# The adaLN gate's multiply-accumulates spread over twelve of sixteen column tiles, with fewer buffers

## The chip, the cores and the metric

One NeuronCore of a Trainium2 chip runs the whole program. The time is that of one execution on the device in microseconds (us), the median of several runs. Engines in the text: TensorE (PE in the rows, PEld its weight loads), VectorE (DVE), ScalarE (ACT), GpSimd (POOL), and SyncE (SP), which issues the DMAs one after the other.

## The reference

One layer of a hybrid sequence model runs on 640 tokens (512 latent, 128 context), 2048 channels wide. The part around the change:

```python
mod = jax.nn.silu(cond) @ p['ada_w'] + p['ada_b']
shift, scale, gate = jnp.split(mod, 3, axis=-1)
xm = rms_norm(x, p['norm_g']) * (1 + scale[:, None]) + shift[:, None]
# mixer: z = xm @ w_in, two scans, then
y_a = (y_rwkv * silu(g_a)) @ p['w_out_a']
y_b = ((h_f + h_bk) * silu(g_b)) @ p['w_out_b']
merged = jax.nn.sigmoid(m_a) * y_a + jax.nn.sigmoid(m_b) * y_b
out = merged @ p['w_out']
x = x + gate[:, None] * out
```

The condition `cond` is one vector for the latent tokens and one for the context tokens, so `gate` is a product of a 2048 x 2048 matrix with two vectors. It is needed only after the last product.

## The kernel before

Everything lies with channels on the 128 partitions and the 640 tokens along the row. All products run in a split form: weights and data are each parted into a high and a low half, and three matmuls (high x high, high x low, low x high) make one product. A weight block `wr` of 128 x 512 comes in by DMA (`fetch`, L297); ScalarE copies each half-tile of 256 columns to `wh` (L309), GpSimd subtracts to get `wl` (L310). `split` keeps five such half-tiles ahead of TensorE, and there are three `wr` buffers. `piece` (L327 in it) issues the matmuls of one block of 128 rows of the weight and then calls `tick`, which advances the generators in the list `side` by one step each. A product of eight blocks so gives eight ticks. The schedule is written out by hand: each engine executes its instructions in the order in which this code emits them.

The stage of the change is that of the sixteen merged column tiles, n = 0 to 15. For each n two old tiles `thx` of 128 x 640 (the stored tanh of the merge gates) are loaded (L1347, L1348), then come the product b(n) of eight blocks with `w_b`, its eviction L1350 on VectorE, the product a(n) with `w_a`, its eviction L1352, the sum L1353, the copy to the high half `xh` on ScalarE (L1355) and the subtraction to the low half `xl` on VectorE (L1356). Two PSUM buffers `pj` hold the products. The two tiles `xh`, `xl` of each n are the data of the last product with `w_o`, which follows the stage.

Ahead of the stage two merge-gate products run; the second half of the last one is evicted by ScalarE into `g` (L1234) six ticks later, inside b(0).

The generator `gates` runs at the side of this stage. It works out the adaLN gate as 64 pairs of multiply-accumulates on VectorE: four quarters h of the 2048 inputs, sixteen tiles n of 128 outputs. For a pair a tile `gws` of 128 x 512 of the transposed weight (256 KB, `ada_g`) is loaded into a ring (L1300), and VectorE multiplies it with the Silu of the condition `cb` (128 copies of 512 inputs for each of two conditions, L1304 loads it, L1309 applies Silu on ScalarE) and sums along the row: L1314 for the first condition, L1316 for the second. Each profile row of them is followed by a short read of the accumulator. A pair takes two ticks, so a tile of the stage has eight pairs, and the gate runs over eight tiles. Its buffers lie in the pool `gp`, on the bytes that the second half of the `xh`, `xl` tiles takes up later. At n = 8 what is left of the generator is emitted at once and the pool is closed.

Of the kernel before, what the change touches and what calls it, by code (L numbers as in the profile page):

```python
# [9 lines left out]
F32 = mybir.dt.float32  # L10
F32R = mybir.dt.float32r
AF = mybir.ActivationFunctionType
ALU = mybir.AluOpType
# [3 lines left out]
P = 128  # L17
D = 2048
KT = D // P
# [16 lines left out]
GK = D // 4  # L36
# [14 lines left out]
X3 = (3, 2, 2, 2, 3, 1, 2, 1)  # L51
NI = (1, 2, 1, 1)

BI, BP, EP = 7, 0.8, 0.5
RMS_EPS = 1e-6
GN_EPS = 64e-5
DECAY = math.exp(-0.5)
# [77 lines left out]
def step_kernel(ctx: ExitStack, tc: tile.TileContext, xt, w_in, w_a, w_b, w_o, ws, lw2, ada_w, ada_g, ada_b, cond, condr, gains,  # L135
                par, gw, s0, cst, y_out, s_out, h_out):
    nc = tc.nc
    V, S, G, PE = nc.vector, nc.scalar, nc.gpsimd, nc.tensor
# [65 lines left out]
    side, back, front, waiting = [], [], [], []  # L204
# [12 lines left out]
    def step(queue):  # L217
        while queue:
            try:
                next(queue[0])  # L220
                return
            except StopIteration:
                queue.pop(0)
# [10 lines left out]
    def idle(n):  # L234
        for _ in range(n):
            yield
# [31 lines left out]
    for i in range(NT):  # L268
        n = NM[i] if i < NT - 1 else 2 * KT - nm - M_AFTER
# [61 lines left out]
    def product(key, xs, cuts=(0, HT, T), ps=None):  # L331
        js = jobs[key]
        if ps is None:
            ps = ps2()
            hs = [(ps[:, s], a, b) for s, (a, b) in enumerate(zip(cuts, cuts[1:]))]
        else:
            hs = [(p, a, b) for p, a, b in zip(ps, cuts, cuts[1:])]
        for n, j in enumerate(js):
            piece(j, xs, hs, 4 * n, 4 * len(js))
        return ps  # L340

    def halves(t):
        return t[:, :T].rearrange("p (a b) -> p a b", a=2)
# [16 lines left out]
    def operand(pool, k):  # L360
        xs.append((pool.tile([P, T], F32R, name=f"xh{k}"), pool.tile([P, T], F32R, name=f"xl{k}")))
# [36 lines left out]
    with tc.tile_pool(name="start", bufs=1) as st, tc.tile_pool(name="ps", bufs=2, space=PSUM) as sp:  # L398
# [34 lines left out]
        for s in range(2):  # L433
            h = slice(s * HT, (s + 1) * HT)
# [270 lines left out]
    with tc.tile_pool(name="rwkv", bufs=1) as rp:  # L705
# [523 lines left out]
        def merge_gate(j, pool=mpool, bufs=1):  # L1229
            ps = product(("m", j), xs)  # L1230

            def half(s):
                t = pool.tile([P, HT], F32, tag="g", name="g", bufs=bufs)
                S.activation(t, ps[:, s, :HT], AF.Tanh, scale=0.5)  # L1234
                later(1, lambda: nc.sync.dma_start(thm[j][:, s * HT:(s + 1) * HT], t))

            half(0)
            later(6, lambda: half(1))
# [22 lines left out]
    with tc.tile_pool(name="outp", bufs=1) as op:  # L1261
        ab_ = {}

        def branches():
            todo = [(n, src[i], i) for n, src in (("b", ybd), ("a", yad)) for i in range(NT)]
            held = []

            def load():
                if todo:
                    n, src, i = todo.pop(0)  # L1270
                    t = op.tile([P, T], F32, tag="yr", name="yr", bufs=6)
                    nc.sync.dma_start(t, src)
                    held.append((n, i, t))

            for _ in range(5):
                load()
            yield from idle(BI)
            while held:
                n, i, t = held.pop(0)
                h, lo = op.tile([P, T], F32R, name=f"y{n}h{i}"), op.tile([P, T], F32R, name=f"y{n}l{i}")  # L1280
                S.activation(h, t, AF.Copy)
                V.tensor_tensor(lo, t, h.bitcast(F32), ALU.subtract)
                ab_[n, i] = (h, lo)
                load()
                yield

        def gates():

            gs = op.tile([P, 4, KT, 2], F32, name="gs")
            cb = [gp.tile([P, 2, GK], F32, name=f"cb{h}") for h in range(4)]  # L1290
            ring = [gp.tile([P, GK], F32, name=f"gws{n}") for n in range(6)]
            junk = gp.tile([P, GK], F32, name="junk")
            todo = [(h, n) for h in range(4) for n in range(KT)]
            held = []

            def load():
                if todo:
                    h, n = todo.pop(0)
                    w = ring[(h * KT + n) % len(ring)]
                    nc.sync.dma_start(w, ada_g[h, n])  # L1300
                    held.append((h, n, w))

            for h in range(4):
                nc.sync.dma_start(cb[h], condr[h:h + 1].to_broadcast([P, 2, GK]))  # L1304
            for _ in range(len(ring) - 1):
                load()
            yield from idle(4)
            for h in range(4):
                S.activation(cb[h], cb[h], AF.Silu)  # L1309
                yield  # L1310
            while held:
                h, n, w = held.pop(0)
                load()
                V.scalar_tensor_tensor(junk, w, 1.0, cb[h][:, 0], ALU.mult, ALU.mult, accum_out=gs[:, h, n, 0:1])  # L1314
                yield
                V.scalar_tensor_tensor(w, w, 1.0, cb[h][:, 1], ALU.mult, ALU.mult, accum_out=gs[:, h, n, 1:2])  # L1316
                yield
            V.tensor_tensor(gs[:, 0:2], gs[:, 0:2], gs[:, 2:4], ALU.add)
            V.tensor_tensor(gs[:, 0], gs[:, 0], gs[:, 1], ALU.add)
            V.tensor_tensor(mod[:, 2], gs[:, 0], adb[:, 2].unsqueeze(2).to_broadcast([P, KT, 2]), ALU.add)  # L1320

        pace[:] = [0.0, BP]
        side.append(branches())
        for k in range(M_AFTER):
            merge_gate(2 * KT - M_AFTER + k, op, 4)
        while side:
            step(side)

        pace[:] = [0.0, 1.0]
        xstack.close()  # L1330
        del xs[:]
        first_half = ctx.enter_context(tc.tile_pool(name="merged0", bufs=1, side="right"))
        for k in range(KT // 2):
            operand(first_half, k)
        gstack = ExitStack()
        gp = gstack.enter_context(tc.tile_pool(name="gp", bufs=1, side="right"))
        side.append(gates())
        for n in range(KT):
            if n == KT // 2:
                while side:  # L1340
                    step(side)
                gstack.close()
                second_half = ctx.enter_context(tc.tile_pool(name="merged1", bufs=1, side="right"))
                for k in range(KT // 2, KT):
                    operand(second_half, k)
            ta, tb = (op.tile([P, T], F32, tag="yr", name="thx", bufs=6) for _ in range(2))
            nc.sync.dma_start(ta, thm[n])  # L1347
            nc.sync.dma_start(tb, thm[KT + n])  # L1348
            ps = product(("b", n), [ab_["b", i] for i in range(NT)])
            V.scalar_tensor_tensor(halves(tb), halves(tb), 1.0, ps[:, :, :HT], ALU.add, ALU.mult)  # L1350
            ps = product(("a", n), [ab_["a", i] for i in range(NT)])
            V.scalar_tensor_tensor(halves(ta), halves(ta), 1.0, ps[:, :, :HT], ALU.add, ALU.mult)  # L1352
            V.tensor_tensor(ta, ta, tb, ALU.add)  # L1353
            h, lo = xs[n]
            S.activation(h, ta, AF.Copy)  # L1355
            V.tensor_tensor(lo, ta, h.bitcast(F32), ALU.subtract)  # L1356
# [79 lines left out]
```

## Time and profile before

| | |
|---|---|
| median of 3 runs | 2256.55 us (2256.01 to 2258.0) |
| the profiled execution | 2254.77 us, its span 2253.0 us |
| TensorE busy | 2111.6 us, 94% of the span |
| VectorE busy | 1365.5 us, 61% |
| ScalarE busy | 976.4 us, 43% |
| GpSimd busy | 874.2 us, 39% |
| mean granted TensorE clock | 0.975 of full |
| moved by DMA | 281.64 MB |

The span runs from the first to the last instruction of the profiled execution; 1.77 us lie around it. Busy shares are means over the whole program, whose stages have different limits, so they do not tell what bounds one stage. TensorE's busy time holds pipelined matmuls with modelled ends.

### The profile page before, as it was taken

How to read it: one execution, taken by the hardware profiler on the slowest of the kernel's cores; microseconds unless marked ns; L12 is line 12 of the kernel's file. 1: busy time of each engine (PE TensorE's matmuls, PEld its weight loads, DVE VectorE, ACT ScalarE, POOL GpSimd, SP SyncE). 2: the span in 40 equal slices, each digit the busy share in tenths (PEclk: the TensorE clock that was granted, in tenths of full speed). 3: DMA queues.
4: the chain of work that ended last, by engine and by line, in shares of the span. 5: the costliest groups of instructions: out<-in, count | busy, mean ns of one | idle time of the engine just before them, and what ended most of it. 6: DMA issues, size and time to landing. Idle time of an engine off the chain costs nothing.

```text
span 2253.0 us, 47526 instructions
## 1 busy us (share of the span) xinstructions
PE 2111.6 (94%) x18236; PEld 1968.6 (87%) x18236; DVE 1365.5 (61%) x2665; ACT 976.4 (43%) x2264; POOL 874.2 (39%) x1164
## 2 busy tenths in 40 slices
PE   3999999999999998999989989989999888999997
PEld 2789999998888898888988988979888888999997
DVE  5555765687656676676466666764614798223364
ACT  4346776543444344334433444344335212234554
POOL 1244554553333433323333333334324445443343
PEclk8999999999999999999999999999999999999999
DMA  9953333323322223223222222232224765344474
GB/s 336 348 170 127 127 114 121 101 93 88 94 75 83 70 81 95 62 75 97 80 83 71 80 86 68 71 110 73 86 77 161 254 207 176 117 145 155 156 236 153
DMA packets 203507, 281.64 MB, mean 125 GB/s; under 512 B 69360, under 2 KB 91056, under 8 KB 202768
## 3 DMA queue, kind: packets, MB, share of 16 engines
q1 hardware_dynamic: 202832, 277.38, 38.5%
q8 instruction: 144, 2.36, 0.4%
q0 software_dynamic: 448, 1.23, 0.2%
q14 instruction: 83, 0.68, 0.1%
HBM read 237.70 MB, written 39.85 MB: 123 GB/s over the span
## 4 chain that ended last, share of the span: by engine, by line
PE 72%; DVE 19%; DMA 5%; issue 2%; ACT 1%; SPq 1%; POOL 0%; DVEq 0%; ACTq 0%; POOLq 0%
PE pj L327 53%; DVE tmp L1072 3%; DVE xi L1074 3%; DVE junk L1314 3%; PE rw L563 3%; DVE gws L1316 2%; PE rw L479 2%; PE rw L930 2%; DVE st L954 1%; PE pj L479 1%; PE ada L381 1%; PE rw L1153 1%; PE rw L1141 1%; PE rw L948 1%; PE rw L1166 1%
## 5 line engine op out<-in xcount | busy, mean ns | idle before, releaser
L310 POOL TENSOR_TENSOR wl<-wr,wh 128x256 fp32r<-128x256 f32 x922 | 789.6, 865 | 1289.0 <-ACT wh L309 1202.7
L327 PE MATMUL pj<-xh,wh 128*128 128x320 f32 (+2 forms) x2976 | 762.3, 323 | 2.6 <-ACT wh L309 2.5
L327 PE MATMUL pj<-xh,wl 128*128 128x320 f32 (+2 forms) x2976 | 726.2, 311 | 2.0 <-DVE wl L310 1.5
L327 PE MATMUL pj<-xl,wh 128*128 128x320 f32 (+2 forms) x2976 | 724.8, 311 | 0.0
L309 ACT ACTIVATE wh<-wr 128x256 fp32r<-128x256 f32 x1048 | 421.3, 413 | 521.5 <-PE pj L327 394.6
L327 PEld LDWEIGHTS pj<-xh,wh 128*128 128x128 f32 x2976 | 503.3, 190 | 34.5 <-issue 14.2
L327 PEld LDWEIGHTS pj<-xh,wl 128*128 128x128 f32 x2976 | 513.5, 190 | 4.0 <-DVE wl L310 2.5
L327 PEld LDWEIGHTS pj<-xl,wh 128*128 128x128 f32 x2976 | 513.8, 190 | 0.1
L1072 DVE TENSOR_TENSOR tmp<-xn,xi 104x30 f32<-104x30 f32 (+14 forms) x240 | 101.7, 424 | 82.3 <-ACT xn L1067 75.7
L1001 DVE COPY sv<-rw 64x128 f32<-64x128 f32 x80 | 23.6, 295 | 199.3 <-ACT sv L1000 198.1
L310 DVE TENSOR_TENSOR wl<-wr,wh 128x256 fp32r<-128x256 f32 x126 | 58.1, 462 | 126.1 <-ACT wh L309 126.0
L1074 DVE TENSOR_TENSOR xi<-xi,tmp 104x30 f32<-104x30 f32 (+14 forms) x240 | 99.9, 416 | 8.2
L327 PE MATMUL pj<-ybh,wh 128*128 128x320 f32 x256 | 62.5, 327 | 21.7 <-DVE thx L1350 21.7
L327 PEld LDWEIGHTS pj<-ybh,wh 128*128 128x128 f32 x256 | 45.9, 202 | 23.5 <-issue 23.5
L1314 DVE SCALAR_TENSOR_TENSOR junk<-gws,cb 128x512 f32<-128x512 f32 x64 | 61.5, 960 | 6.4 <-DMA gws<-ada_g 6.4
L954 DVE TENSOR_TENSOR st<-rw,c 64x512 f32<-64x512 f32 (+1 forms) x96 | 57.6, 600 | 12.4 <-PE rw L948 10.2
L327 PE MATMUL pj<-yah,wh 128*128 128x320 f32 x256 | 59.2, 313 | 6.1 <-DVE thx L1350 4.1
L327 PE MATMUL pj<-ybh,wl 128*128 128x320 f32 x256 | 61.8, 324 | 0.0
L327 PE MATMUL pj<-ybl,wh 128*128 128x320 f32 x256 | 61.8, 324 | 0.0
L327 PE MATMUL pj<-yah,wl 128*128 128x320 f32 x256 | 59.4, 313 | 0.9 <-POOL wl L310 0.9
L1316 DVE SCALAR_TENSOR_TENSOR gws<-gws,cb 128x512 f32<-128x512 f32 x64 | 58.4, 913 | 2.2
L1355 ACT ACTIVATE xh<-thx 128x640 fp32r<-128x640 f32 x16 | 11.8, 740 | 109.8 <-DVE thx L1353 103.4
(766 smaller groups left out, 3102.2 us busy)
## 6 DMA issues: line engine op xcount, KB each, us to landing
wr<-w_in SPq DMA_DIRECT2D x312, 256.0 KB
adaw<-ada_w SPq DMA_DIRECT2D x64, 512.0 KB
wr<-w_o SPq DMA_DIRECT2D x128, 256.0 KB
gws<-ada_g SPq DMA_DIRECT2D x64, 256.0 KB
thl<-th SPq DMA_DIRECT2D x32, 320.0 KB
th<-thl SPq DMA_DIRECT2D x32, 320.0 KB
thm<-g SPq DMA_DIRECT2D x64, 160.0 KB
thx<-thm SPq DMA_DIRECT2D x32, 320.0 KB
```

The costliest lines, as they stand in the source:

```text
L309: S.activation(h, r, AF.Copy)
L310: lows[pos[1] % len(lows)].tensor_tensor(lo, r, h.bitcast(F32), ALU.subtract)
L327: PE.matmul(p[:, :t1 - t0], w, x[:, t0:t1], start=(k == 0 and a == 0), stop=(k == nk - 1 and a == 2))
L479: PE.matmul(p[:, :HT], u[:, w], x[:, t], start=new, stop=end)
L563: PE.matmul(p, a, b, start=(n == 0), stop=(n == 2))
L930: PE.matmul(pa[hd(e), x:x + P], z.bk[d][hd(e), n, e], st4s[d][hd(e), n, e].rearrange("p a t -> p (a t)"), start=True, stop=True)
L954: V.tensor_tensor(st4s[d][so, n0:n0 + nn, e], pb[so, :m].rearrange("p (c a t) -> p c a t", a=2, t=CH), mb[so], ALU.mult)
L1001: V.tensor_copy(sv[hd(1), a, 1], src[hd(1), b])
L1072: V.tensor_tensor(t, xn[:NV, j, j + 1:].unsqueeze(2).to_broadcast([NV, m, j]), xi[:NV, j, :j].unsqueeze(1).to_broadcast([NV, m, j]), ALU.mult)
L1074: V.tensor_tensor(xi[:NV, j + 1:, :j], xi[:NV, j + 1:, :j], t, ALU.add)
L1314: V.scalar_tensor_tensor(junk, w, 1.0, cb[h][:, 0], ALU.mult, ALU.mult, accum_out=gs[:, h, n, 0:1])
L1316: V.scalar_tensor_tensor(w, w, 1.0, cb[h][:, 1], ALU.mult, ALU.mult, accum_out=gs[:, h, n, 1:2])
```

## The change

The generator takes three ticks for a pair instead of two (`GI = (2, 2)`: two steps after the second multiply-accumulate, for even and for odd n), and the stage gives it twelve tiles instead of eight. The `xh`, `xl` tiles are parted into twelve and four, and the gate's buffers lie on the bytes of the last four. They hold four `gws` instead of six and two `cb` instead of four: the first condition is loaded and put through Silu at the start, the next ones during the quarter before. The first multiply-accumulate follows the first Silu without a step between. Lines below the change have numbers higher by seven in the changed code (L1350 is L1357 there).

```diff
--- before.py
+++ after.py
@@ -51,7 +51,7 @@
 X3 = (3, 2, 2, 2, 3, 1, 2, 1)
 NI = (1, 2, 1, 1)
 
-BI, BP, EP = 7, 0.8, 0.5
+BI, BP, EP, GI = 7, 0.8, 0.5, (2, 2)
 RMS_EPS = 1e-6
 GN_EPS = 64e-5
 DECAY = math.exp(-0.5)
@@ -1287,8 +1287,8 @@
         def gates():
 
             gs = op.tile([P, 4, KT, 2], F32, name="gs")
-            cb = [gp.tile([P, 2, GK], F32, name=f"cb{h}") for h in range(4)]
-            ring = [gp.tile([P, GK], F32, name=f"gws{n}") for n in range(6)]
+            ring = [gp.tile([P, GK], F32, name=f"gws{n}") for n in range(4)]
+            cbs = []
             junk = gp.tile([P, GK], F32, name="junk")
             todo = [(h, n) for h in range(4) for n in range(KT)]
             held = []
@@ -1300,21 +1300,28 @@
                     nc.sync.dma_start(w, ada_g[h, n])
                     held.append((h, n, w))
 
-            for h in range(4):
-                nc.sync.dma_start(cb[h], condr[h:h + 1].to_broadcast([P, 2, GK]))
+            def conditions():
+                if len(cbs) < 4:
+                    cbs.append(gp.tile([P, 2, GK], F32, tag="cb", name="cb", bufs=2))
+                    h = len(cbs) - 1
+                    nc.sync.dma_start(cbs[-1], condr[h:h + 1].to_broadcast([P, 2, GK]))
+
+            conditions()
             for _ in range(len(ring) - 1):
                 load()
             yield from idle(4)
-            for h in range(4):
-                S.activation(cb[h], cb[h], AF.Silu)
-                yield
+            S.activation(cbs[0], cbs[0], AF.Silu)
             while held:
                 h, n, w = held.pop(0)
                 load()
-                V.scalar_tensor_tensor(junk, w, 1.0, cb[h][:, 0], ALU.mult, ALU.mult, accum_out=gs[:, h, n, 0:1])
-                yield
-                V.scalar_tensor_tensor(w, w, 1.0, cb[h][:, 1], ALU.mult, ALU.mult, accum_out=gs[:, h, n, 1:2])
-                yield
+                if n == 2:
+                    conditions()
+                elif n == 12 and h < 3:
+                    S.activation(cbs[-1], cbs[-1], AF.Silu)
+                V.scalar_tensor_tensor(junk, w, 1.0, cbs[h][:, 0], ALU.mult, ALU.mult, accum_out=gs[:, h, n, 0:1])
+                yield
+                V.scalar_tensor_tensor(w, w, 1.0, cbs[h][:, 1], ALU.mult, ALU.mult, accum_out=gs[:, h, n, 1:2])
+                yield from idle(GI[n % 2])
             V.tensor_tensor(gs[:, 0:2], gs[:, 0:2], gs[:, 2:4], ALU.add)
             V.tensor_tensor(gs[:, 0], gs[:, 0], gs[:, 1], ALU.add)
             V.tensor_tensor(mod[:, 2], gs[:, 0], adb[:, 2].unsqueeze(2).to_broadcast([P, KT, 2]), ALU.add)
@@ -1329,20 +1336,20 @@
         pace[:] = [0.0, 1.0]
         xstack.close()
         del xs[:]
-        first_half = ctx.enter_context(tc.tile_pool(name="merged0", bufs=1, side="right"))
-        for k in range(KT // 2):
-            operand(first_half, k)
+        merged0 = ctx.enter_context(tc.tile_pool(name="merged0", bufs=1, side="right"))
+        for k in range(KT - 4):
+            operand(merged0, k)
         gstack = ExitStack()
         gp = gstack.enter_context(tc.tile_pool(name="gp", bufs=1, side="right"))
         side.append(gates())
         for n in range(KT):
-            if n == KT // 2:
+            if n == KT - 4:
                 while side:
                     step(side)
                 gstack.close()
-                second_half = ctx.enter_context(tc.tile_pool(name="merged1", bufs=1, side="right"))
-                for k in range(KT // 2, KT):
-                    operand(second_half, k)
+                merged1 = ctx.enter_context(tc.tile_pool(name="merged1", bufs=1, side="right"))
+                for k in range(KT - 4, KT):
+                    operand(merged1, k)
             ta, tb = (op.tile([P, T], F32, tag="yr", name="thx", bufs=6) for _ in range(2))
             nc.sync.dma_start(ta, thm[n])
             nc.sync.dma_start(tb, thm[KT + n])
```

VectorE's order in the first tile, from the first to the last instruction of n = 0 after the earlier stage. Names are those of the text above, with the buffer's number; the wait list names the engines and DMA lanes that a row waits for. Before:

```order
L1350 SCALAR_TENSOR_TENSOR thx_21523<-thx_21523,pj_21526 128x640 [waits DMAHW7_49,DVE_49,PE_49]
L1314 SCALAR_TENSOR_TENSOR junk_21549,gs_21538<-gws0_21543,cb0_21539 128x512 [waits DMAHW5_49,Activation_49]
L1316 SCALAR_TENSOR_TENSOR gws0_21543,gs_21538<-gws0_21543,cb0_21539 128x512 [waits DVE_49]
L1314 SCALAR_TENSOR_TENSOR junk_21549,gs_21538<-gws1_21544,cb0_21539 128x512 [waits DMAHW6_49]
L1316 SCALAR_TENSOR_TENSOR gws1_21544,gs_21538<-gws1_21544,cb0_21539 128x512 [waits DVE_49]
L1314 SCALAR_TENSOR_TENSOR junk_21549,gs_21538<-gws2_21545,cb0_21539 128x512 [waits DMAHW7_49]
L1316 SCALAR_TENSOR_TENSOR gws2_21545,gs_21538<-gws2_21545,cb0_21539 128x512 [waits DVE_49]
L1314 SCALAR_TENSOR_TENSOR junk_21549,gs_21538<-gws3_21546,cb0_21539 128x512 [waits DMAHW0_49]
L1316 SCALAR_TENSOR_TENSOR gws3_21546,gs_21538<-gws3_21546,cb0_21539 128x512 [waits DVE_49]
L1352 SCALAR_TENSOR_TENSOR thx_21522<-thx_21522,pj_21625 128x640 [waits PE_49]
L1353 TENSOR_TENSOR thx_21522<-thx_21522,thx_21523 128x640 [waits DVE_49]
L1356 TENSOR_TENSOR xl0_21504<-thx_21522,xh0_21503 128x640 [waits Activation_49]
```

The changed kernel, the same place:

```order
L1321 SCALAR_TENSOR_TENSOR junk_21551,gs_21546<-gws0_21547,cb_21552 128x512 [waits DMAHW2_49,PE_49,Activation_49]
L1323 SCALAR_TENSOR_TENSOR gws0_21547,gs_21546<-gws0_21547,cb_21552 128x512 [waits DVE_49]
L1321 SCALAR_TENSOR_TENSOR junk_21551,gs_21546<-gws1_21548,cb_21552 128x512 [waits DMAHW3_49]
L1357 SCALAR_TENSOR_TENSOR thx_21531<-thx_21531,pj_21534 128x640 [waits DMAHW7_49,PE_49]
L1323 SCALAR_TENSOR_TENSOR gws1_21548,gs_21546<-gws1_21548,cb_21552 128x512 [waits DVE_49]
L1321 SCALAR_TENSOR_TENSOR junk_21551,gs_21546<-gws2_21549,cb_21552 128x512 [waits DMAHW4_49]
L1323 SCALAR_TENSOR_TENSOR gws2_21549,gs_21546<-gws2_21549,cb_21552 128x512 [waits DVE_49]
L1321 SCALAR_TENSOR_TENSOR junk_21551,gs_21546<-gws3_21550,cb_21552 128x512 [waits DMAHW6_49]
L1323 SCALAR_TENSOR_TENSOR gws3_21550,gs_21546<-gws3_21550,cb_21552 128x512 [waits DVE_49]
L1359 SCALAR_TENSOR_TENSOR thx_21530<-thx_21530,pj_21625 128x640 [waits PE_49]
L1360 TENSOR_TENSOR thx_21530<-thx_21530,thx_21531 128x640 [waits DVE_49]
L1363 TENSOR_TENSOR xl0_21504<-thx_21530,xh0_21503 128x640 [waits Activation_49]
```

Three multiply-accumulates now stand ahead of the first eviction (L1357, before L1350), and five instead of eight between it and the second (L1359). In the later tiles ten or eleven stand where there were sixteen.

ScalarE's order at the start of the stage, from the last `wh` ahead of the gate's first step. Before:

```order
L309 ACTIVATE wh_21565<-wr_21386 128x256 [waits PE_49,Pool_49]
L309 ACTIVATE wh_21583<-wr_21437 128x256 [waits DMAHW4_49,PE_49,Pool_49]
L1309 ACT_TABLE_LOAD
L1309 ACTIVATE cb0_21539<-cb0_21539 128x1024 [waits DMAHW1_49]
L1234 ACTIVATE g_21600<-pj_21300 128x320
L1309 ACTIVATE cb1_21540<-cb1_21540 128x1024 [waits DMAHW2_49]
L309 ACTIVATE wh_21603<-wr_21437 128x256 [waits PE_49,Pool_49]
L1309 ACTIVATE cb2_21541<-cb2_21541 128x1024 [waits DMAHW3_49]
L1309 ACTIVATE cb3_21542<-cb3_21542 128x1024 [waits DMAHW4_49]
L309 ACTIVATE wh_21626<-wr_21483 128x256 [waits DMAHW5_49,PE_49,Pool_49]
```

The changed kernel:

```order
L309 ACTIVATE wh_21563<-wr_21386 128x256 [waits PE_49,Pool_49]
L309 ACTIVATE wh_21581<-wr_21437 128x256 [waits DMAHW4_49,PE_49,Pool_49]
L1313 ACT_TABLE_LOAD
L1313 ACTIVATE cb_21552<-cb_21552 128x1024 [waits DMAHW1_49]
L1234 ACTIVATE g_21600<-pj_21300 128x320
L309 ACTIVATE wh_21603<-wr_21437 128x256 [waits PE_49,Pool_49]
L309 ACTIVATE wh_21626<-wr_21483 128x256 [waits DMAHW5_49,PE_49,Pool_49]
L309 ACTIVATE wh_21643<-wr_21483 128x256 [waits PE_49,Pool_49]
L309 ACTIVATE wh_21666<-wr_21567 128x256 [waits DMAHW5_49,PE_49,Pool_49]
```

The copy `g` stands behind the first Silu in both; the other three Silus, which stood among the next three instructions, are gone from here.

TensorE's order where the product b(0) ends and a(0) begins (`yb`, `ya` are the two branches' data). Before:

```order
L327 MATMUL pj_21526<-ybh6_21324,wl_21480 128x320
L327 MATMUL pj_21526<-ybh7_21342,wh_21479 128x320 x2
L327 MATMUL pj_21526<-ybl7_21343,wh_21479 128x320 [waits DVE_49]
L327 MATMUL pj_21526<-ybl7_21343,wh_21479 128x320
L327 MATMUL pj_21526<-ybh7_21342,wl_21480 128x320 x2
L327 MATMUL pj_21625<-yah0_21354,wh_21527 128x320 [waits DVE_49,Activation_49]
```

The changed kernel:

```order
L327 MATMUL pj_21534<-ybh6_21324,wl_21480 128x320
L327 MATMUL pj_21534<-ybh7_21342,wh_21479 128x320 x2
L327 MATMUL pj_21534<-ybl7_21343,wh_21479 128x320 [waits DVE_49]
L327 MATMUL pj_21534<-ybl7_21343,wh_21479 128x320
L327 MATMUL pj_21534<-ybh7_21342,wl_21480 128x320 x2
L327 MATMUL pj_21625<-yah0_21354,wh_21535 128x320 [waits Activation_49]
```

The first matmul of a(0) waited for VectorE and ScalarE and now waits for ScalarE only; the product after it, b(1), waited for ScalarE only and now waits for VectorE and ScalarE. Which of the two PSUM buffers a product gets is chosen when the program is built.

## Rows read from the trace of the kernel before

**Rows 1.** The page, part 4: shares of the chain that ended last.

```profile
PE 72%; DVE 19%; DMA 5%; issue 2%; ACT 1%; SPq 1%; POOL 0%; DVEq 0%; ACTq 0%; POOLq 0%
```

**Rows 2.** Windows: us, busy PE, PEld, DVE, ACT, POOL, granted clock, DMA share, GB/s.

```profile
1832.13:1869.17 37.04, 30.72 (x192) 29.72 (x192) 34.81 (x75) 7.06 (x18) 18.18 (x16) 0.95 0.65 207
1930.80:1958.96 28.16, 28.16 (x194) 28.16 (x193) 6.59 (x9) 7.72 (x19) 12.32 (x16) 1.00 0.37 122
1746.90:1757.20 10.30, 6.20 (x32) 6.23 (x33) 0.82 (x1) 4.35 (x6) 0.86 (x2) 0.83 1.01 361
```

**Rows 3.** Timeline of DVE in one gate tile: start, length, instruction [idle before].

```profile
1832.13 0.81 DVE L1350 SCALAR_TENSOR_TENSOR thx<-thx,pj 128x640 f32<-128x640 f32 x1
1832.86 0.68 DVE L1314 SCALAR_TENSOR_TENSOR junk<-gws,cb 128x512 f32<-128x512 f32 x1
...
1838.24 0.81 DVE L1352 SCALAR_TENSOR_TENSOR thx<-thx,pj 128x640 f32<-128x640 f32 x1
...
1841.46 1.24 DVE L1314 SCALAR_TENSOR_TENSOR junk<-gws,cb 128x512 f32<-128x512 f32 x1
...
1850.65 0.81 DVE L1350 SCALAR_TENSOR_TENSOR thx<-thx,pj 128x640 f32<-128x640 f32 x1
```

**Rows 4.** Timeline of DVE in the stage's second half, without the gate.

```profile
1923.76 0.82 DVE L1352 SCALAR_TENSOR_TENSOR thx<-thx,pj 128x640 f32<-128x640 f32 x1 [6.22 <-PE pj L327]
...
1930.80 0.82 DVE L1350 SCALAR_TENSOR_TENSOR thx<-thx,pj 128x640 f32<-128x640 f32 x1 [3.72 <-PE pj L327]
...
1944.88 0.82 DVE L1350 SCALAR_TENSOR_TENSOR thx<-thx,pj 128x640 f32<-128x640 f32 x1 [3.73 <-PE pj L327]
```

**Rows 5.** Timeline of PE: first matmuls of a(0), b(1), a later b, and w_o.

```profile
1751.00 0.53 PE L327 MATMUL pj<-yah,wh 128*128 128x320 f32 x2 [4.11 <-DVE thx L1350]
...
1759.64 0.46 PE L327 MATMUL pj<-ybh,wh 128*128 128x320 f32 x2
...
1851.60 0.53 PE L327 MATMUL pj<-ybh,wh 128*128 128x320 f32 x2 [2.67 <-DVE thx L1350]
...
2008.04 0.32 PE L327 MATMUL pj<-xh,wh 128*128 128x350 f32 x1
```

**Rows 6.** Timeline of POOL: a gate tile, then an undisturbed tile.

```profile
1841.07 9.10 POOL L310 TENSOR_TENSOR wl<-wr,wh 128x256 fp32r<-128x256 f32 x8 [9.42 <-DMA thx<-thm]
...
1926.60 2.46 POOL L310 TENSOR_TENSOR wl<-wr,wh 128x256 fp32r<-128x256 f32 x3 [3.61 <-ACT wh L309]
1929.30 0.74 POOL L310 TENSOR_TENSOR wl<-wr,wh 128x256 fp32r<-128x256 f32 x1 [0.23 <-ACT wh L309]
1931.05 0.74 POOL L310 TENSOR_TENSOR wl<-wr,wh 128x256 fp32r<-128x256 f32 x1 [1.01 <-ACT wh L309]
```

**Rows 7.** Timeline of SP's DMA issues: start of the stage, and one weight load.

```profile
1746.80 2.00 SPq L1304 DMA_DIRECT2D cb<-condr  x4
1748.85 4.10 SPq L1300 DMA_DIRECT2D gws<-ada_g  x5
...
1843.33 0.33 SPq L297 DMA_DIRECT2D wr<-w_b  x1
```

**Rows 8.** Timeline of ACT: start of the stage, and the copy after that load.

```profile
1752.62 1.06 ACT L1309 ACTIVATE cb<-cb 128x1024 f32<-128x1024 f32 x1 [6.25 <-DMA cb<-condr]
1753.59 0.42 ACT L1234 ACTIVATE g<-pj 128x320 f32<-128x320 f32 x1
...
1846.41 0.42 ACT L309 ACTIVATE wh<-wr 128x256 fp32r<-128x256 f32 x1 [2.53 <-DMA wr<-w_b]
```

**Rows 9.** Timeline of DVE at the start of the stage.

```profile
1750.03 0.82 DVE L1350 SCALAR_TENSOR_TENSOR thx<-thx,pj 128x640 f32<-128x640 f32 x1 [5.71 <-DMA thx<-thm]
1757.20 0.69 DVE L1314 SCALAR_TENSOR_TENSOR junk<-gws,cb 128x512 f32<-128x512 f32 x1 [6.35 <-DMA gws<-ada_g]
```

**Rows 10.** Waits of SP from 1757 to 1907: us in total, times, longest us.

```profile
SPq L297 <- POOL wl L310: 45.4, 20, 5.8
```

**Rows 11.** Waits of all engines from 1740 to 1910, the same columns.

```profile
DVE junk L1314 <- DMA gws<-ada_g: 6.4, 1, 6.4
```

## The prediction

> **What bounds the kernel now.** I read the page first: TensorE is busy nearly everywhere, but the chain that ended last gives VectorE 19% [rows 1], and two of its lines there are the gate's multiply-accumulates, L1314 and L1316. They all lie in one stage, the sixteen merged column tiles, so I read that stage by itself. While the gate runs, two tiles take 37.04 us and VectorE is busy for 34.81 of them; once it is over, two tiles take 28.16 us with TensorE busy throughout [rows 2]. So the first half of the stage is bound by VectorE at 18.52 us a tile (two L1350 apart, [rows 3]), the second by TensorE at 14.08 (two L1350 apart, [rows 4]). In the first half TensorE idles 2.67 us in each tile, released by L1350 [rows 5]: the next b product needs the PSUM buffer that L1350 empties, and L1350 stands behind eight multiply-accumulates.
>
> What a tile costs VectorE comes from [rows 3]. L1350 takes 0.73 us (to the next start). From L1352 to the first gate instruction after L1356 it is 3.22 us, ScalarE's L1355 included. That is 3.95 us of evictions. Eight multiply-accumulates take 5.38 us between 1832.86 and 1838.24, that is 0.6725 each; the other eight take 9.19 us between 1841.46 and 1850.65, that is 1.149 each. The slow eight coincide with the eight wl subtractions of GpSimd, which start at 1841.07 and take 9.10 us [rows 6]. So a wl that meets the gate costs VectorE (9.19 - 5.38) / 8 = 0.476 us. It costs GpSimd too: 1.14 us each there, 0.74 alone [rows 6].
>
> **The change, part by part.**
>
> *Pauses.* A pair of multiply-accumulates now takes three ticks instead of two, and a tile has sixteen ticks: 5.33 pairs, 10.67 instructions a tile instead of 16, over twelve tiles instead of eight (the 64th pair is left for the boundary). VectorE then has 10.67 x 0.6725 + 3.95 = 11.13 us a tile if no wl meets the gate, and 11.13 + 8 x 0.476 = 14.94 if all eight do. TensorE's 14.08 lies between: it decides if at most 6.2 of the eight meet. Three wl come in a burst behind the copy xh, the others about 1.75 us apart [rows 6], and some meet evictions or a free VectorE instead. I take seven (the burst, and most of the others, since the gate fills most of a tile): 14.46 us, 0.38 more than TensorE.
>
> That surplus does not reach TensorE at once. In an undisturbed tile L1352 starts at 1923.76, the first wl behind xh at 1926.60 and is done by 1927.42 (2.46 / 3 = 0.82 each); the a product whose first half-tile it is begins at 1930.80 [rows 4, 6] and wants it after four matmuls, 0.59 us later (48 matmuls in 7.04 us). VectorE may thus be 4.0 us late, 3.6 if that wl is slowed by 0.4. The PSUM buffers give more, nearly a product of 7.04 us. Over eleven tiles after the first the lag is 11 x 0.38 = 4.2 us, less 3.6: **a loss of 0.6, say 1 us**. With all eight meeting, 11 x 0.86 - 3.6 = 5.9 us.
>
> *Start of the stage.* Now four condition loads (2 MB) go out at 1746.80, in front of five gate loads [rows 7]; the first condition is there at 1752.62 [rows 8], the first gate tile at 1757.20 [rows 9]. From then VectorE is the bound. TensorE waited 4.11 us for the first L1350 and began a(0) at 1751.00, b(1) at 1759.64 [rows 5]; the clock was granted at 0.83 of full there [rows 2], which is why a(0) took 8.64 us and not 7.04. With one condition, three loads fewer lie ahead. Two things change by the order of instructions. VectorE now has three multiply-accumulates in front of the first eviction, and a(0) no longer waits for VectorE at all: it takes the other PSUM buffer, which ScalarE empties with g (L1234), and g stands behind the one Silu. So a(0) starts at the Silu's start (1752.62 at the latest; at the earliest 1.1 us sooner, since the data of L1350 landed by 1750.03 [rows 9] and 0.5 MB at the stage's 361 GB/s [rows 2] takes 1.45) + 0.97 to g [rows 8] + 0.57 (g's 0.42, and 0.15 to hand over, as from the end of L1350 to 1751.00): 1753.0 to 1754.2, I take 1753.6. That is 2.6 us later than before. The eviction must be done only for b(1): gate tiles at about 1753 and 1754, three multiply-accumulates of 0.67 to 1.15, so it starts at 1755 to 1757.5, long before a(0) ends at 1753.6 + 8.64 = 1762.2.
>
> *From there.* Fifteen tiles at 14.08 are 211.2 us: the last product of the stage begins to follow at 1973.4. Before it was 2008.04 [rows 5]. That is **34.6 us**, less 1 for the lag: 33.6. Put otherwise: from 1759.64 the fifteen tiles took 248.4 us and need 211.2; of the 37.2 between, the later start takes 2.6 back.
>
> *Ring of four.* The load for pair m+3 waits for pair m-1. Between lie three pairs, 3 x 1.345 = 4.0 us at their fastest, 5.9 at the mean of the sum. A load of the same size issued at 1843.33 released ScalarE at 1846.41, 3.1 us [rows 7, 8], with DMA at 65% and 207 GB/s [rows 2]. The new rate is about the same: 1 MB of weights, 0.66 of thx, 5.33 x 0.26 of gate in 14.08 us make 218 GB/s. I take nothing; the bound is a rival.
>
> *Two conditions.* Three Silus (1.06 us) move among ScalarE's wh. ScalarE is busy 7.06 of 37.04 us [rows 2], and the wh behind it is for a half-tile four ahead: nothing. If that cover were gone it is 3.2 us in all. Their loads add 3 x 0.5 MB over twelve tiles, 9 GB/s. Memory: the last four tiles' bytes are wanted only at the thirteenth tile, and the last pair is behind by then: nothing, at most its 2.3 us.
>
> **Sum.** The profiled run took 2254.77 us, 1.78 less than the median of 2256.55. 2254.77 - 33.6 + 1.78 = **2223 us**.
>
> **A rule against it.** In the trace one wl takes 0.476 us from VectorE [rows 3, 6]. The Trainium skill, "SBUF — State Buffer", section "SBUF: two separate sides", says that a VectorE instruction with two inputs in SBUF and a GpSimd instruction hold their shared ports for their whole length, and that the other is fully blocked. By that a tile before would be 16 x 0.6725 + 3.95 + 8 x 0.74 = 20.6 us; the trace has 18.52 and does not agree in size.
>
> **Rivals.**
> 1. *VectorE stays the bound:* all eight wl meet the gate, 14.94 us. Speaks for it that they did so before; against it that five come spaced. Loss 5.9 instead of 1: 2228 us. 17%.
> 2. *The first eviction holds a(0) after all* (the trace of before shows it waiting there, the new order not). With gate data only as late as 1757, three multiply-accumulates and 0.97, a(0) would start at about 1760: 6.5 us more, 2229.5. 7%.
> 3. *The ring is too short:* SyncE is in order, and its weight loads wait for wl up to 5.8 us [rows 10]. A gate load behind such a one comes 5.8 + 3.1 = 8.9 us after its buffer is free, 3.0 later than the 5.9 of three pairs. If that happens in every second tile, VectorE has 14.46 + 1.5 = 15.96: 11 x 1.88 - 3.6 = 17.1 us lost, 2239.5. Against it: after its first wait of 6.4 us VectorE never waited for gate data [rows 11], though with five loads ahead. 8%.
> 4. *A wl blocks VectorE for its whole 0.74 us* once it comes singly: 11.13 + 8 x 0.74 = 17.05 us, 11 x 2.97 - 3.6 = 29 us lost, 2251. Against it: the 0.476 measured. 3%. The Trainium skill's page above states the rule by which it would come so.
> 5. *Slower:* rival 3 in every tile and twice. The gain is gone when (34.6 + 3.6) / 11 = 3.5 us a tile are lost, 3.1 us beyond my sum, one such load in every tile; two make 11 x 6.4 - 3.6 = 67 us and 2289. 3%.
>
> That the pauses change nothing, because VectorE runs ahead of them, is no case: it cannot pass L1350 or L1352 before TensorE is done, so no more than a tile's share is done in a tile.
>
> **How the numbers follow.** My forecast, TensorE the bound and a loss of 0 to 3 us, has 62%: 2221 to 2225.5. Rivals 1 and 2 reach to 2230, with their own uncertainty of 3 us to 2233; rivals 3, 4 and 5 with 14% stay outside. Below, no lag and an a(0) at 1753.0 give 2221.3, and 1.5 us for run and unknowns 2219.5. About 0.2% (4.5 us) is what a measurement here can tell: faster 0.95, same 0.02 (part of rival 4), slower 0.03.
>
> **What would show it.** Right: evictions of b 14.08 us apart from the second tile on; a(0) released by ScalarE near 1753.6; VectorE idle at some L1357 or L1359 for TensorE; no VectorE wait for gate data after the first tile; the stage's end near 1973. Lag: L1359 later and later behind its product, up to 4 us. Wrong: TensorE waiting in every tile for L1357, xh's wl or wh; VectorE waiting for DMA in the middle; the clock below full there.

## The result, and the profile after

The changed kernel takes 2223.08 us, the median of four runs (2219.61 to 2225.43), against 2257.28 (2256.01 to 2259.22) for the kernel before on the same chip: a ratio of 0.9847 [0.9829, 0.9864]. It is faster by 1.5%. The forecast was 2223.0, range 2219.5 to 2233.

The profiled execution took 2224.06 us with a span of 2222.3, 30.7 us below the profiled 2254.77 of before. On the page of the changed kernel the chain that ended last still gives VectorE the same 19% as in [rows 1] (the chain may follow either of two engines that are nearly level; the windows tell them apart better). The two multiply-accumulates, now L1321 and L1323, keep their 64 pairs, but their means are 1055 and 961 ns, where they were 960 and 913: 84 of the 128 take over 0.8 us, where it was 67, since the gate now runs beside the wl of twelve tiles instead of eight.

```profile
PE 71%; DVE 19%; DMA 4%; issue 3%; ACT 2%; SPq 1%; POOL 1%; DVEq 0%; ACTq 0%; POOLq 0%
...
L1321 DVE SCALAR_TENSOR_TENSOR junk<-gws,cb 128x512 f32<-128x512 f32 x64 | 67.5, 1055 | 10.1 <-ACT cb L1313 10.1
...
L1323 DVE SCALAR_TENSOR_TENSOR gws<-gws,cb 128x512 f32<-128x512 f32 x64 | 61.5, 961 | 1.9
```

Windows of the changed kernel, columns as in [rows 2]: a(0), ten tiles with the gate, and a stretch after it.

```profile
1754.57:1764.42 9.85, 9.85 (x50) 9.85 (x51) 7.77 (x18) 1.81 (x5) 4.30 (x5) 0.72 0.63 197
1779.66:1924.58 144.92, 144.27 (x980) 143.55 (x980) 134.88 (x257) 38.94 (x93) 85.96 (x80) 1.00 0.70 224
1932.00:1960.00 28.00, 28.00 (x193) 28.00 (x192) 7.53 (x10) 8.04 (x19) 13.12 (x18) 1.00 0.41 133
```

With the gate running, TensorE is now busy for 144.27 of 144.92 us at the full clock; in [rows 2] it was 30.72 of 37.04 at 0.95. VectorE is busy for 93% of the same stretch. The DMA moved 224 GB/s (the estimate was 218).

TensorE's timeline: a(0)'s first matmuls, the first of b(1), b(2), b(3) and b(12), and w_o.

```profile
1754.57 0.90 PE L327 MATMUL pj<-yah,wh 128*128 128x320 f32 x2 [8.13 <-ACT g L1234]
1755.27 0.73 PE L327 MATMUL pj<-yal,wh 128*128 128x320 f32 x2
...
1764.22 0.46 PE L327 MATMUL pj<-ybh,wh 128*128 128x320 f32 x2
...
1778.30 0.46 PE L327 MATMUL pj<-ybh,wh 128*128 128x320 f32 x2
...
1792.38 0.46 PE L327 MATMUL pj<-ybh,wh 128*128 128x320 f32 x2
...
1920.49 0.46 PE L327 MATMUL pj<-ybh,wh 128*128 128x320 f32 x2
...
1977.33 0.32 PE L327 MATMUL pj<-xh,wh 128*128 128x350 f32 x1
```

Beside [rows 5]: a(0) is released by ScalarE's g, not by VectorE, after 8.13 us instead of 4.11; b products follow each other at 14.08 us without the 2.67 us gap (the first six; later ones take up to 14.61); and the stage ends at 1977.33 instead of 2008.04, the whole 30.7 us of the profiled run. Of these, 0.8 us lie ahead of the stage, where nothing was changed (b(0) begins at 1738.45 instead of 1739.23); behind the stage both runs need 245.0 us to their end.

VectorE's timeline: the first multiply-accumulate, the evictions of the first tile, and then L1359 of the tiles n = 1 and n = 11.

```profile
1754.23 0.69 DVE L1321 SCALAR_TENSOR_TENSOR junk<-gws,cb 128x512 f32<-128x512 f32 x1 [10.06 <-ACT cb L1313]
...
1757.25 0.81 DVE L1357 SCALAR_TENSOR_TENSOR thx<-thx,pj 128x640 f32<-128x640 f32 x1
...
1764.42 0.82 DVE L1359 SCALAR_TENSOR_TENSOR thx<-thx,pj 128x640 f32<-128x640 f32 x1 [1.98 <-PE pj L327]
...
1779.66 0.81 DVE L1359 SCALAR_TENSOR_TENSOR thx<-thx,pj 128x640 f32<-128x640 f32 x1
...
1924.58 0.81 DVE L1359 SCALAR_TENSOR_TENSOR thx<-thx,pj 128x640 f32<-128x640 f32 x1
```

L1359 is the second eviction of a tile and can start when its a product ends, which is when the next b product begins. The first starts 0.20 us behind that (1764.42 beside 1764.22), the second 1.36 (1779.66 beside 1778.30), the one of 1924.58 4.09 (beside 1920.49). VectorE falls behind, slowly: 144.92 us for ten tiles are 14.49 each.

ScalarE's timeline around the first Silu, one tile of GpSimd's, and the waits of all engines between 1740 and 1985:

```profile
1753.14 1.06 ACT L1313 ACTIVATE cb<-cb 128x1024 f32<-128x1024 f32 x1 [6.75 <-DMA cb<-condr]
1754.10 0.42 ACT L1234 ACTIVATE g<-pj 128x320 f32<-128x320 f32 x1
```

```profile
1884.05 8.65 POOL L310 TENSOR_TENSOR wl<-wr,wh 128x256 fp32r<-128x256 f32 x8 [6.00 <-PE pj L327]
```

```profile
DVE junk L1321 <- ACT cb L1313: 10.1, 1, 10.1
...
PE pj L327 <- ACT g L1234: 8.1, 1, 8.1
...
PE pj L327 <- POOL wl L310: 1.0, 4, 0.3
...
PE pj L327 <- DVE thx L1357: 0.4, 1, 0.4
```

The first condition was there only at 1753.14, later than the 1752.62 of [rows 8], although three fewer condition loads were issued behind it. Eight wl take 8.65 us, so they still meet the gate. VectorE has no wait for gate data in the list (6.4 us in [rows 11]), only the one for the Silu. After that start the list has TensorE waiting for an eviction once, 0.4 us; of its four waits for a wl two lie in the gate's tiles, 0.3 us each.

### The profile page after: what moved, and what is told of

It is laid out like the page before. It is cut to its first block, busy times and chain, and to the rows that moved or that the text cites. A ratio compares the mean times of both kernels' runs of the same rounds, so it can differ in the third digit from the quotient of the medians.

```text
span 2222.3 us, 47521 instructions
## 1 busy us (share of the span) xinstructions
PE 2102.0 (95%) x18236; PEld 1960.5 (88%) x18236; DVE 1373.5 (62%) x2665; ACT 976.0 (44%) x2264; POOL 876.1 (39%) x1164
## 4 chain that ended last, share of the span: by engine, by line
PE 71%; DVE 19%; DMA 4%; issue 3%; ACT 2%; SPq 1%; POOL 1%; DVEq 0%; ACTq 0%; POOLq 0%
PE pj L327 52%; DVE tmp L1072 3%; DVE xi L1074 3%; PE rw L563 3%; DVE junk L1321 2%; PE rw L479 2%; PE rw L930 2%; DVE gws L1323 1%; DVE st L954 1%; PE ada L381 1%; PE pj L479 1%; PE rw L1153 1%; PE rw L1141 1%; PE rw L1166 1%; PE rw L948 1%
## 5 line engine op out<-in xcount | busy, mean ns | idle before, releaser
L1321 DVE SCALAR_TENSOR_TENSOR junk<-gws,cb 128x512 f32<-128x512 f32 x64 | 67.5, 1055 | 10.1 <-ACT cb L1313 10.1
L1323 DVE SCALAR_TENSOR_TENSOR gws<-gws,cb 128x512 f32<-128x512 f32 x64 | 61.5, 961 | 1.9
L327 PE MATMUL pj<-yal,wh 128*128 128x320 f32 x256 | 59.2, 313 | 0.0
L1000 ACT ACTIVATE sv<-rw 64x128 f32<-64x128 f32 x80 | 21.7, 271 | 74.7 <-PE rw L1153 68.9
```

The costliest lines, as they stand in the source:

```text
L327: PE.matmul(p[:, :t1 - t0], w, x[:, t0:t1], start=(k == 0 and a == 0), stop=(k == nk - 1 and a == 2))
L1321: V.scalar_tensor_tensor(junk, w, 1.0, cbs[h][:, 0], ALU.mult, ALU.mult, accum_out=gs[:, h, n, 0:1])
L1323: V.scalar_tensor_tensor(w, w, 1.0, cbs[h][:, 1], ALU.mult, ALU.mult, accum_out=gs[:, h, n, 1:2])
```

## The experiments

The theory: the pauses made room for TensorE, since VectorE's load in a tile fell from 18.52 us to about TensorE's own 14.08; the start and the buffers are minor. Rivals: the start or the buffers did it; or VectorE remains the bound because GpSimd's wl keep slowing it. I compare the stage's length as well as the times, from the first matmul of b(0) to the first of w_o: before 1739.23 to 2008.04, 268.8 us; changed kernel 1738.45 to 1977.33, 238.9.

**Without the pauses** (on the changed kernel):

```diff
-BI, BP, EP, GI = 7, 0.8, 0.5, (2, 2)
+BI, BP, EP, GI = 7, 0.8, 0.5, (1, 1)
```

> The changed kernel with two ticks a pair again: ring of four, two conditions and the new start stay. Theory (pauses): VectorE is the bound again with 16 multiply-accumulates a tile, 18.5 us between first evictions; its chain starts 3.0 us earlier than before with the first gate data (1754.2 for 1757.2) and has one eviction more in it (0.7), so 2.3 us are gained: about 2254 us, 2250 to 2257. Rival (the smaller start burst and the freed a(0) bring most of it, the pauses little): 2223 to 2230, first evictions 14 to 15 us apart. If a ring of four alone harms: above 2257, with VectorE waiting for gate data.

Measured: 2251.04 us, ratio to before 0.9979 [0.9968, 0.9989]; stage 265.0 us. VectorE's timeline and a window of five tiles of this kernel:

```profile
1830.86 0.81 DVE L1357 SCALAR_TENSOR_TENSOR thx<-thx,pj 128x640 f32<-128x640 f32 x1
...
1849.37 0.81 DVE L1357 SCALAR_TENSOR_TENSOR thx<-thx,pj 128x640 f32<-128x640 f32 x1
```

```profile
1793.83:1886.39 92.56, 77.21 (x480) 74.84 (x480) 86.98 (x181) 19.33 (x47) 46.10 (x41) 0.94 0.68 219
```

Tiles are 18.51 us apart again, VectorE is full (94%) and TensorE idles 15.4 of 92.6 us. So the pauses carry 265.0 - 238.9 = 26.1 of the stage's 29.9 us, the new start and buffers together 3.8. That 3.8 holds where VectorE is the bound and only its own earlier start counts. In the changed kernel the new start is a loss: from b(0) to b(1) 25.8 us pass instead of 20.4, and from b(1) to w_o 213.1 instead of 248.4, so 5.4 of 35.3 us gained are given back.

**Shorter pauses alone** (on the kernel before, with its six gate buffers, four conditions and its start; 2.5 ticks a pair over ten tiles):

```diff
-BI, BP, EP = 7, 0.8, 0.5
+BI, BP, EP, GI = 7, 0.8, 0.5, (1, 2)
...
-                yield
+                yield from idle(GI[n % 2])
...
-        for k in range(KT // 2):
+        for k in range(KT - 6):
```

> The kernel before with its own buffers (ring of six, four conditions) and start, but 2.5 ticks a pair over ten tiles. Theory (the sum for VectorE in a tile): 12.8 multiply-accumulates x 0.6725 + 3.95 + 7 to 8 meetings x 0.476 = 15.9 to 16.4 us a tile, VectorE the bound over nine tiles: the stage ends near 1989 and the time is 2235 to 2243. Rival (ring and conditions count, not the pauses): 2250 to 2257. Rival (any pause puts TensorE at its own 14.08): 2221 to 2226.

Measured: 2237.17 us, 0.9918 [0.9897, 0.994]; stage 250.3 us. VectorE's timeline, first and last of nine evictions L1350:

```profile
1774.63 0.81 DVE L1350 SCALAR_TENSOR_TENSOR thx<-thx,pj 128x640 f32<-128x640 f32 x1
...
1902.37 0.81 DVE L1350 SCALAR_TENSOR_TENSOR thx<-thx,pj 128x640 f32<-128x640 f32 x1
```

Eight tiles in 127.74 us are 15.97 each, as the sum wanted: VectorE is still the bound, for two tiles more, and the result lies between the two kernels. Pauses over more tiles, without the new start and the fewer buffers, give what the load per tile says.

**The same multiply-accumulates without GpSimd beside them.** In the gate's tiles wl becomes a plain copy by ScalarE (so the low half of these weights is wrong), on the kernel before and then on the changed one:

```diff
...
-            lows[pos[1] % len(lows)].tensor_tensor(lo, r, h.bitcast(F32), ALU.subtract)
+            if apart[0]:
+                S.activation(lo, r, AF.Copy)
+            else:
+                lows[pos[1] % len(lows)].tensor_tensor(lo, r, h.bitcast(F32), ALU.subtract)
...
```

On the kernel before, eight tiles:

> The kernel before, but in the eight gate tiles wl is a plain copy by ScalarE instead of GpSimd's subtraction (so the low half of the weights is wrong there): GpSimd is idle beside the gate. Theory (eight wl a tile take 0.476 us each from VectorE): every multiply-accumulate takes 0.67 us, a tile 16 x 0.6725 + 3.95 = 14.7 us instead of 18.5, and the time falls by about 30 us, to 2223 to 2229, with no pause at all. Rival (the slow multiply-accumulates are slow for another reason, DMA writes or the phase of the tile): half of them still take 1.15 us and the time stays at 2253 to 2260.

Measured: 2227.16 us, 0.9879 [0.986, 0.9898]; stage 241.8 us. The tile view of junk (shortest, median and longest ns) and a window of six tiles:

```profile
L1318 DVE SCALAR_TENSOR_TENSOR junk<-gws,cb x64: 683/686/1221, 1762.2 to 1880.8; 128x512 f32<-128x512 f32 x64
```

```profile
1782.34:1870.73 88.39, 86.46 (x581) 84.99 (x581) 81.68 (x219) 35.16 (x102) 0.00 (x0) 1.00 0.78 260
```

A tile takes 88.39 / 6 = 14.73 us, and 16 x 0.6725 + 3.95 is 14.71. So with all sixteen multiply-accumulates in every tile but no wl, 27 us of the stage go away. It is not the DMA writes that made half of them slow: the DMA moved more here (260 GB/s, 207 in [rows 2]), and the median is 686 ns. GpSimd's subtractions cost VectorE (18.52 - 14.73) / 8 = 0.474 us each, by taking them away; the prediction had 0.476 from comparing two halves of a tile. The Trainium skill ("SBUF — State Buffer", section "SBUF: two separate sides") has the loser fully blocked while the other holds the ports; by that my estimate would be the 0.74 us of a whole wl [rows 6], and this run does not agree in size.

On the changed kernel, twelve tiles:

> The changed kernel, but in the twelve gate tiles wl is a plain copy by ScalarE (so the low half of the weights is wrong there), and GpSimd is idle beside the gate. Theory (with the pauses TensorE is the bound, and the meetings of wl and gate only make the lag): VectorE falls to 11 to 11.5 us a tile with idle time in front of its evictions, TensorE has 14.08 in every tile, and only the 1.9 us of lost time come back: 2219 to 2224, the stage about 237 us. Rival (the meetings still cost time in the changed kernel as they did before): 10 us or more below the changed kernel, 2205 to 2213.

Measured: 2222.26 us, 0.9848 [0.9833, 0.9862]; stage 235.5 us, where the changed kernel, profiled once more on that chip, had 237.3. A window of ten tiles and 0.6 us, and two evictions L1365 (L1359 in the changed kernel) on VectorE's timeline:

```profile
1779.63:1921.00 141.37, 141.37 (x966) 141.37 (x965) 102.85 (x255) 65.00 (x173) 0.00 (x0) 1.00 0.69 227
```

```profile
1835.95 0.82 DVE L1365 SCALAR_TENSOR_TENSOR thx<-thx,pj 128x640 f32<-128x640 f32 x1 [2.18 <-PE pj L331]
...
1850.03 0.82 DVE L1365 SCALAR_TENSOR_TENSOR thx<-thx,pj 128x640 f32<-128x640 f32 x1 [2.92 <-PE pj L331]
```

Now VectorE waits for TensorE, and TensorE never waits. What was worth 27 us before is worth 1.8 here. Counted from b(1) to w_o, which leaves the uneven start out, it is 213.2 against 211.2 us, that is 2.0: all that VectorE's lag still costs TensorE in the changed kernel. In time it does not show beside the spread of the runs.

**The start, and the changed kernel again.** The first Silu, and with it the gate, comes four ticks later:

```diff
-            yield from idle(4)
+            yield from idle(8)
             S.activation(cbs[0], cbs[0], AF.Silu)
```

> The changed kernel with eight empty steps instead of four ahead of the first Silu, so that the copy g and two more wh stand before it and the first eviction before the gate. a(0) then needs no condition: it should start at about 1746 instead of 1754.6, without the 8.1 us wait and the slow clock. Theory (VectorE is busy without a gap from the first gate data on, TensorE can only run ahead of it by some 5 us): the first gate instruction stays at about 1754, the first L1359 comes 5 us or more behind its product, and only 3 to 6 us are gained: 2217 to 2220. Rival (the wait of a(0) is lost time of TensorE and comes back whole): 10 to 11 us, 2212 to 2213.

Measured: 2219.67 us (2218.11 to 2221.21), 0.9842 [0.9825, 0.9859]; stage 233.4 us. TensorE's timeline: the first matmuls of a(0), a(1), b(13) and w_o; then VectorE's first eviction, first multiply-accumulate and first L1359, and ScalarE's copy behind it.

```profile
1746.01 0.46 PE L327 MATMUL pj<-yah,wh 128*128 128x320 f32 x2
...
1761.80 0.56 PE L327 MATMUL pj<-yah,wh 128*128 128x320 f32 x2 [1.55 <-ACT wh L309]
...
1929.43 0.53 PE L327 MATMUL pj<-ybh,wh 128*128 128x320 f32 x2 [1.21 <-DVE thx L1357]
...
1971.74 0.32 PE L327 MATMUL pj<-xh,wh 128*128 128x350 f32 x1
```

```profile
1749.76 0.82 DVE L1357 SCALAR_TENSOR_TENSOR thx<-thx,pj 128x640 f32<-128x640 f32 x1 [5.87 <-PE pj L327]
1753.58 0.69 DVE L1321 SCALAR_TENSOR_TENSOR junk<-gws,cb 128x512 f32<-128x512 f32 x1 [3.00 <-ACT cb L1313]
...
1758.99 0.82 DVE L1359 SCALAR_TENSOR_TENSOR thx<-thx,pj 128x640 f32<-128x640 f32 x1
```

```profile
1760.70 0.74 ACT L1362 ACTIVATE xh<-thx 128x640 fp32r<-128x640 f32 x1 [4.68 <-DVE thx L1360]
```

a(0) no longer waits and runs at full pitch: b(1) begins at 1753.05, 11.2 us earlier than in the changed kernel. But only 5.5 us of it reach the end. The gate starts hardly sooner (1753.58 beside 1754.23), so the first L1359 (1758.99) comes 5.9 us after the end of its product (1753.05), and ScalarE's copy xh and the wh that a(1) wants come behind it. TensorE waits 1.55 us for that wh and runs part of a(1) at a granted clock of 0.53 (1763.63 to 1767.23); b(1) and a(1) take 18.0 us, and later TensorE waits at evictions. To set the remainder apart, the changed kernel and this one ran once more, side by side:

> The changed kernel once more, on the chip of the next three: 2220 to 2226 us, the stage from the start of b(0) to the first product with w_o 239 us long.

> The kernel with the later gate once more beside the changed one, to tell the two apart. Theory (a(0) no longer waits 8.1 us, of which the lag behind VectorE takes about half back): its stage is about 5 us shorter, 233 to 235 us, and its median 3 to 6 us below that of the changed kernel. Rival (the smaller median was another chip's): within 1.5 us of it.

Measured: changed kernel 2224.79 us (2222.43 to 2226.16), 0.9854 [0.9838, 0.9871], stage 237.3; later gate 2221.48 (2220.23 to 2221.82), 0.9842 [0.9827, 0.9857], stage 234.3. The later gate is 3.3 us or 0.15% ahead. The two sets of runs don't overlap and the stage is 3.1 us shorter, but the intervals against before do overlap, and 0.15% is below the 0.2% that counts as told apart here. It is the fastest version that ran, by little. The changed kernel's stage was 238.9 us in one profiled run and 237.3 in the other; the difference lies ahead of b(1), and from b(1) to w_o they took 213.1 and 213.2.

**A ring of three** (on the changed kernel):

```diff
-            ring = [gp.tile([P, GK], F32, name=f"gws{n}") for n in range(4)]
+            ring = [gp.tile([P, GK], F32, name=f"gws{n}") for n in range(3)]
```

> The changed kernel with a ring of three. Theory (a load lands some 3.1 us after its issue, and two pairs between its issue and its use take 2.7 us at their fastest and 3.9 at the mean): VectorE waits for gate data now and then, some tenths of a us a tile; its 14.5 us a tile grow to at most 15, TensorE loses 0 to 6 us: 2223 to 2229. Rival (the ring's length is what the stage hangs on, rival 3 of the prediction): 1.5 us or more a tile, above 2235.

Measured: 2224.44 us (2221.87 to 2224.93), 0.9854 [0.9839, 0.9869], the changed kernel's own time on that chip; stage 237.4. A window of ten tiles:

```profile
1780.48:1925.48 145.00, 144.26 (x980) 143.53 (x979) 134.97 (x257) 38.95 (x93) 86.08 (x80) 1.00 0.68 222
```

14.50 us a tile, and VectorE's only wait on the gate is again the first Silu's; the waits of some tenths of a us a tile that were expected did not come. A buffer less than the change's four costs nothing, so the fall from six to four cannot have cost anything either.

## Why the prediction was right, step by step

**The mechanism** held: VectorE's load per tile was the bound, spreading the gate brought it near TensorE's, and taking the pauses away loses 26.1 of 29.9 us. Two of the signs named for it did not come: evictions of b came 14.42 us apart in the mean of ten tiles, not 14.08, and after the first tile VectorE never waited for TensorE while the gate ran. VectorE so stays the slower by 0.4 us a tile, as the sum's own 14.46 has it and "TensorE the bound" does not, and the gain rests on the surplus not reaching TensorE at once. Of the 33.6 us that the profiled run was to gain by the end of this stage, 30.7 came. The median lies 1 us below the changed kernel's profiled run (the sum had put it 1.78 above), so that 2223.08 came so near to 2223.0 is luck; the steps missed by three terms of one us each:

- *a(0) starts* at 1754.57, not 1753.6: the order of instructions was read rightly (released by ScalarE's g, the first eviction at 1757.25 as forecast between 1755 and 1757.5), but the condition was there at 1753.14, and the sum had put that no later than 1752.62. That with three condition loads fewer it could only come sooner was assumed and is wrong: the first condition is issued ahead of them. From its issue to the Silu 6.50 us passed here and 5.82 before; in the other runs it was 5.5 and 6.7 with four conditions, 5.8 to 6.3 with one. One reading was taken for a bound.
- *a(0) lasts* 9.65 us, not 8.64. The sum copied the length from before, where the wait ahead of it was half as long.
- *The lag* cost 1977.33 - 1764.22 - 211.2 = 1.9 us, not 1. The tile was sized well: 14.49 us where the sum had 14.46, and its seven meetings are in the trace: seven multiply-accumulates of each of these tiles take over 1 us. But not because some wl come spaced and miss: from the fourth tile on all eight come in one block (8.65 us above), and the eviction L1357 takes one place in it. The first of the eleven tiles has eight slow ones and took 15.24 us (1764.42 to 1779.66). In all VectorE fell behind by 160.16 - 11 x 14.08 = 5.3 us instead of 4.2; 1.4 of it reached TensorE by 1920.49, 3.9 stood as lag, and 0.5 followed.

**The tolerance** of 3.6 us was right for the wait that it was worked out for, and another wait cost nearly as much. TensorE's waits, and the evictions that they follow, in the changed kernel:

```profile
1885.17 0.56 PE L327 MATMUL pj<-yah,wl 128*128 128x320 f32 x2 [0.26 <-POOL wl L310]
...
1906.33 0.53 PE L327 MATMUL pj<-ybh,wh 128*128 128x320 f32 x2 [0.36 <-DVE thx L1357]
...
1928.53 0.57 PE L327 MATMUL pj<-yah,wl 128*128 128x320 f32 x2 [0.25 <-POOL wl L310]
```

```profile
1881.22 0.81 DVE L1359 SCALAR_TENSOR_TENSOR thx<-thx,pj 128x640 f32<-128x640 f32 x1
...
1905.37 0.81 DVE L1357 SCALAR_TENSOR_TENSOR thx<-thx,pj 128x640 f32<-128x640 f32 x1
```

Behind the two L1359 that come 4.1 us after their products (1881.22 beside 1877.12, and 1924.58 beside 1920.49) the next a product waits for a wl and loses 0.5 us, so 3.6 us were free; with L1359 up to 3.6 us late no product waits for a wl. But the first eviction, L1357, comes later behind its product than L1359, up to 6.6 us for n = 10 (1905.37 beside 1898.77), and the next b product needs its PSUM buffer: b(11) begins 0.52 us late and b(8) 0.19. So the PSUM buffers give 6.1 us, not nearly 7.04, and the sum had counted no lag for L1357. Of the 1.9 us the two waits for wl make 1.0, those for L1357 with their slower first matmuls 0.9. The changed kernel with wl on ScalarE, where there is no lag, has no product above 7.04 us after a(0).

**The buffers** cost nothing, as said: neither four gate tiles nor two conditions show as a wait.

**The rivals.** 1, all eight wl meet: one tile came above it (15.24 beside 14.94), the mean did not; its loss of 5.9 us is 1.9. In its weaker sense, that VectorE remains the slower of the two by a little, it is true, and the run without wl prices it at 1.8 to 2.0 us. 2, the first eviction holds a(0): no, ScalarE's g does. 3 and 5, the ring: no, a shorter one changes nothing (rival 3's time is 2239.1 by its own terms, not 2239.5). 4, a wl blocks for its whole length: a tile would be 17.05 us; it is 14.49, and 0.474 us is what a wl costs when it is taken away.

## What to carry to other kernels

Work it out per tile, not over the span: side work that fits under the bound engine on average still stalls it wherever it is issued densely, and pauses that bring the side engine's load per tile down to the bound engine's time give the stall back. A small surplus per tile is harmless as long as its sum stays below how late the side engine may be (here 3.6 us for one eviction and 6.1 for the other, read from the time between its result and the instruction that uses it): every result that is waited for has its own. Before pricing contention as lost, ask which engine is the bound: the same GpSimd interference was worth 27 us of stage when VectorE was, and 2 when the pauses had brought VectorE's load near TensorE's.

## What was not expected of the hardware

**The clock after a wait.** Windows of a(0), columns as in [rows 2], two of the kernel before and two of the changed one:

```profile
1751.70:1754.90 3.20, 3.20 (x13) 3.20 (x13) 0.00 (x0) 2.28 (x4) 0.00 (x0) 0.50 1.02 398
1754.90:1759.64 4.74, 4.74 (x34) 4.74 (x34) 2.40 (x5) 3.01 (x6) 2.48 (x3) 0.99 1.04 393
```

```profile
1754.57:1760.07 5.50, 5.50 (x20) 5.50 (x21) 5.43 (x12) 0.98 (x3) 2.83 (x3) 0.50 0.42 141
1760.07:1764.22 4.15, 4.15 (x30) 4.15 (x29) 2.34 (x6) 0.83 (x2) 1.47 (x2) 0.99 0.90 269
```

In the kernel before, a(0) waits 4.11 us and takes 8.64 us: it keeps nearly full pitch for some 0.7 us, and then the granted clock is 0.50, the level of 1.2 GHz, for 3.2. In the changed kernel it waits 8.13 us and is slow from the first matmul (0.70 us to the next pair in the rows at 1754.57 and 1755.27), for 5.5 us. In the others that wait 7.1 to 8.0 us there it is slow from the first matmul too. After 4.81 us (ten tiles) and 4.68 us (wl on ScalarE in the kernel before) a(0) takes 8.57 and 8.65. a(0) takes 9.65 and 8.55 us in the two runs of the changed kernel, 9.51 without the pauses, 9.23 with the ring of three and 8.87 with its wl on ScalarE. In four of these five runs the longer wait was followed by a longer a(0) too, by 0.2 to 1.0 us over the 8.64 of before; between the two runs of one kernel that differed by 1.1 us, so a term of this kind is not known to better than a microsecond.

**An order that moves a buffer.** With VectorE instructions put ahead of the first eviction, a(0) got another PSUM buffer, and so another engine to wait for: ScalarE, whose g stood behind the Silu. With the gate four ticks later g is no longer behind it, and a(0) starts without any wait, 8.6 us sooner. There the first eviction stands ahead of the gate again, at 1749.76, and a(0), begun at 1746.01, does not wait for it; so VectorE's order alone does not decide which buffer a(0) gets, and what does was not shown.
